# The RWKV recurrence: its triangular solver's data in another DRAM order, block tiles that serve four ticks, and loads issued ahead of output stores

## The chip, the cores and the metric

One Trainium2 chip, one of its cores. The metric is the device time of the whole program in microseconds (us), the median of three runs. The core has five engines with a queue each: TensorE (PE, with its weight loads PEld), VectorE (DVE), ScalarE (ACT), GpSimd (POOL) and SyncE (SP), which here only issues DMAs. Each queue runs in order, and an instruction that waits holds up all that stand behind it.

## The reference

A two-layer trunk: RWKV-7 time mixing and a mixture of experts, then differential attention and a second mixture of experts. Only the time mixing is touched. Its core, for each of 16 heads, is a recurrence over 1024 tokens with a 64x64 state:

```python
def step(S, inp):
    r_t, w_t, k_t, v_t, a_t, b_t = inp
    sa = jnp.einsum('bhij,bhj->bhi', S, a_t)
    S = S * w_t[:, :, None, :] + sa[..., None] * b_t[:, :, None, :] + v_t[..., None] * k_t[:, :, None, :]
    return S, jnp.einsum('bhij,bhj->bhi', S, r_t)
_, y = lax.scan(step, S0, (tm(r_h), tm(w_h), tm(k_h), tm(v_h), tm(a_vec), tm(b_vec)))
```

after which y is normalised by head, gets a bonus term, is multiplied by a gate and by `w_o`.

## The kernel before

The recurrence is computed in chunks of 64 tokens. Two heads stand on the 128 partitions as a pair (p = 0 to 7); two pairs make a couple (four of them, c or g below). Within a chunk the recurrence needs the inverse of a triangular 64x64 matrix I - A for every head and chunk. A is split into 32x32 blocks: the inverses D of the two diagonal blocks come from a forward substitution (the solver), and the block C below the diagonal is used as it is, in three products s1, s2, s3 (Q = D X, P2 = C Q, R = D P2 + Q).

Two stages follow one another, written out by hand in one order for all engines (`tc.manual_schedule()`, L1453), so every queue holds its instructions in the order in which the code is written.

*The k stage* (`rwkv_k`, loop over n at L1455, about 300 to 560 us): 16 units of one pair and half the tokens each. Iteration n makes projections for unit n, norms for unit n - 1, and for unit n - 2 the matrices: `prods` (PE, tile `pA`, from `at` and `bk`) and `mask` (DVE, tile `am`). A unit's `am` holds A (stored to `d['A']`, L1578) and a second matrix (L1579). `ei` (stored to `d['rt']`, L1547 and L1549), `bk` (stored at L1533) and `am` have one buffer each, so each store has to be done before the next unit writes the tile. Four DMAs on POOL's queue fill `d['D']` with zeros ahead of the stage (L1408).

*The recurrence* (`Mix.main`, loop over n at L801, about 526 to 910 us): 32 ticks (and two to drain), each of them two chunks of one couple, eight ticks to a couple. Its first two ticks are interleaved with the last two iterations of the k stage (`mb.step`). Tick n issues `first(n)` (products with the tile `rec`, 768 KB, and with `rI`), `turn(n)`, s1 to s5 for tick n - 1, and the serial `chain(n - 2)`. At its end the loads for tick n + 2 are issued on SP: `rec` and four DMAs for the C blocks (`bdC`) in `load`, `bdD` in `load_t`, `rI` in `load_r`. `gn` normalises finished outputs, from tick 6 on, two pieces in four ticks: on PE, ACT, DVE and twice on POOL (L788, L790, tile `gyc`), and ends with a store to `d['y']` (L797).

*The solver* (`solve_gen`) is a generator, of which a few steps at a time are woven into the order (`mb.solve`, `self.solve`). For couple g it loads A from DRAM with 8 DMAs (L592), so that each of the 128 partitions holds one 32x32 block for 8 of the 16 (head, chunk) places, runs 62 small instructions (L601, L604), on DVE for couple 0 and on POOL for 1 to 3, and stores D with 8 DMAs (L611):

```python
nc.sync.dma_start(a[q0:q0 + 16], src[r:r + 32, :, 32 * b:32 * b + 32].rearrange("i u j -> u i j"))
eng.tensor_mul(tv, a[:, s + 1:, s:s + 1].to_broadcast([P, n, s + 1]),
                     t[:, s:s + 1, :s + 1].to_broadcast([P, n, s + 1]))
```

In the k stage only couple 0 is solved (`mb.solve(.., 1)`); couple 1 begins in tick 0, and `self.solved` at n % 8 == 6 makes sure that a couple is through before its ticks come.

Of the kernel before, what the change touches and what calls it, by code (L numbers as in the profile page):

```python
# [18 lines left out]
P = 128  # L19
# [524 lines left out]
class Mix:  # L544
# [32 lines left out]
    def solve_gen(self, g, eng):  # L577


        nc, d, sp = self.nc, self.d, self.sp  # L580
        B = 32
        for _ in range(3):
            yield
        a = sp.tile([P, B, B], F32, name="big", bufs=3)
        t = sp.tile([P, B, B], F32, name="big", bufs=3)
        for y in range(2):
            src = d['A'][g][:, y]
            for b in range(2):
                for h in range(2):
                    q0 = 64 * y + 32 * b + 16 * h  # L590
                    r = 64 * h + 32 * b
                    nc.sync.dma_start(a[q0:q0 + 16], src[r:r + 32, :, 32 * b:32 * b + 32].rearrange("i u j -> u i j"))  # L592
        nc.gpsimd.memset(t, 0.0)
        for _ in range(9):
            yield
        eng.memset(t.rearrange("p i j -> p (i j)")[:, 0:B * B:B + 1], 1.0)
        for s in range(B - 1):
            n = B - 1 - s
            tmp = sp.tile([P, 256], F32, name="so_tmp", bufs=2)
            tv = tmp[:, :n * (s + 1)].rearrange("p (i j) -> p i j", j=s + 1)  # L600
            eng.tensor_mul(tv, a[:, s + 1:, s:s + 1].to_broadcast([P, n, s + 1]),  # L601
                                 t[:, s:s + 1, :s + 1].to_broadcast([P, n, s + 1]))
            yield
            eng.tensor_add(t[:, s + 1:, :s + 1], t[:, s + 1:, :s + 1], tv)  # L604
            yield
        for y in range(2):
            for b in range(2):
                for h in range(2):
                    q0 = 64 * y + 32 * b + 16 * h
                    o = slice(64 * y + 32 * b, 64 * y + 32 * b + 32)  # L610
                    nc.sync.dma_start(d['D'][g][o, h, :, 32 * b:32 * b + 32].rearrange("i u j -> u i j"), t[q0:q0 + 16])  # L611
        yield

    def main(self):
# [58 lines left out]
        def first(n):  # L673
# [6 lines left out]
            t = qp.tile([P, 8, 2 * L], F32, name="XK", bufs=3)  # L680
# [86 lines left out]
        def gn(p, th):  # L767
# [3 lines left out]
            if th == 0:  # L771
                g2[p] = wp.tile([P, P], F32, name=f"g2{p % 2}", bufs=2)
# [6 lines left out]
            yc = wp.tile([P, 512], F32, name="gyc")  # L779
# [125 lines left out]
class Kern:  # L905
# [237 lines left out]
    def rwkv(self, x, A, rows, ada_first, ada_rest, x_rd, moe, em):  # L1143
# [12 lines left out]
        d['A'] = couples('A', [P, 2, NCH, L])  # L1156
        d['D'] = couples('D', [P, 2, NCH, L])
# [231 lines left out]
    def rwkv_k(self, A, d, wp, front, Z, W2, half, kah, col, PLs, sel2, sel8, strict, X, W, strip, mb):  # L1389
# [5 lines left out]
        with ExitStack() as e1:  # L1395
# [59 lines left out]
            if True:  # L1455
                for n in range(18):
# [107 lines left out]
                    mb.solve(solving, 1)  # L1564
# [12 lines left out]
                    if c:  # L1577
                        nc.sync.dma_start(d['A'][pc_ // 2][:, pc_ % 2, 8 * thc:8 * thc + 8, :], c['am'][:, 0])  # L1578
# [599 lines left out]
```

## Time and profile before

| | us |
|---|---|
| median of three runs | 3038.64 |
| the three runs | 3037.49, 3038.64, 3048.1 |
| the profiled execution, its own time | 3041.39 |
| its span (first to last instruction) | 3039.7 |

Over the span PE is busy for 2669.4 us (88%), DVE for 2295.2 (76%), ACT for 1596.5 (53%), POOL for 1050.4 (35%). These shares are averages over stages with different limits; the change is in one stage of some 600 us. A timeline row gives the start in us, the length in us, the engine, the source line, the operation, the tile written and the tiles read, and in brackets how long the engine had been idle and what released it. "acc<-rI,rec" marks the first matmuls of a tick, so the distance between two such rows is a tick's length.

### The profile page before, as it was taken

How to read it: one execution, taken by the hardware profiler on the slowest of the kernel's cores; microseconds unless marked ns; L12 is line 12 of the kernel's file. 1: busy time of each engine (PE TensorE's matmuls, PEld its weight loads, DVE VectorE, ACT ScalarE, POOL GpSimd, SP SyncE). 2: the span in 40 equal slices, each digit the busy share in tenths (PEclk: the TensorE clock that was granted, in tenths of full speed). 3: DMA queues.
4: the chain of work that ended last, by engine and by line, in shares of the span. 5: the costliest groups of instructions: out<-in, count | busy, mean ns of one | idle time of the engine just before them, and what ended most of it. 6: DMA issues, size and time to landing. Idle time of an engine off the chain costs nothing. (4 is left out here: it accounts for less than half of the span.)

```text
span 3039.7 us, 47397 instructions
## 1 busy us (share of the span) xinstructions
PE 2669.4 (88%) x18150; PEld 2088.7 (69%) x18150; DVE 2295.2 (76%) x3328; ACT 1596.5 (53%) x2105; POOL 1050.4 (35%) x786
## 2 busy tenths in 40 slices
PE   6999998588879699999996789989979799999994
PEld 3567766555658588888774577767758688888773
DVE  7895688345555699999996457676687799999996
ACT  5653433244432177777774244444533377777773
POOL 2000554554332222332223537676242223222320
PEclk9999888789998799999998699999989799999997
DMA  7486765755645499999996113233135499999994
GB/s 263 150 266 215 221 184 166 171 139 148 181 122 196 160 369 380 379 373 367 371 365 216 48 39 99 71 92 98 36 117 199 177 376 379 375 376 374 370 366 175
DMA packets 356952, 696.79 MB, mean 229 GB/s; under 512 B 113336, under 2 KB 231408, under 8 KB 307568
## 3 DMA queue, kind: packets, MB, share of 16 engines
q1 hardware_dynamic: 330144, 649.59, 60.9%
q0 software_dynamic: 22080, 42.00, 5.5%
q8 instruction: 145, 2.38, 0.3%
q10 hardware_dynamic: 4496, 2.12, 0.3%
q14 instruction: 87, 0.71, 0.1%
HBM read 612.71 MB, written 110.15 MB: 238 GB/s over the span
## 5 line engine op out<-in xcount | busy, mean ns | idle before, releaser
L1116 DVE TENSOR_TENSOR elo<-eraw,ehi 128x2048 fp32r<-128x2048 f32 x384 | 871.4, 2286 | 73.6 <-ACT ehi L1113 73.2
L1113 ACT ACTIVATE ehi<-eraw 128x2048 fp32r<-128x2048 f32 x384 | 736.0, 1920 | 178.4 <-PE eacc L350 76.5
L393 POOL DMA_INDIRECT x<-ey,gtab x64 | 205.2, 3206 | 842.4 <-DVE ey L388 831.9
L350 PE MATMUL eacc<-ehi,xTl 128*128 128x512 f32 x1024 | 293.0, 398 | 0.0
L350 PE MATMUL eacc<-ehi,xTh 128*128 128x512 f32 x1024 | 284.1, 399 | 5.8 <-ACT ehi L1113 5.8
L350 PE MATMUL eacc<-elo,xTh 128*128 128x512 f32 x1024 | 277.9, 393 | 0.0
L350 PEld LDWEIGHTS eacc<-elo,xTh 128*128 128x128 f32 x1024 | 193.1, 189 | 43.3
L350 PEld LDWEIGHTS eacc<-ehi,xTh 128*128 128x128 f32 x1024 | 188.8, 190 | 44.0 <-ACT ehi L1113 6.6
L350 PEld LDWEIGHTS eacc<-ehi,xTl 128*128 128x128 f32 x1024 | 188.9, 189 | 38.0
L1771 PE MATMUL acc<-axh,w_hi 128*128 128x512 f32 x384 | 172.9, 450 | 8.1 <-ACT axh L1113 5.5
L1771 PE MATMUL acc<-axl,w_hi 128*128 128x512 f32 x384 | 156.9, 409 | 0.0
L1771 PE MATMUL acc<-axh,w_lo 128*128 128x512 f32 x384 | 156.1, 406 | 0.0
L1892 ACT ACTIVATE pr<-sc,mx 128x128 f32<-128x128 f32 (+7 forms) x128 | 94.1, 739 | 83.4 <-DVE mx L1878 41.6
L378 PE MATMUL ey<-elo,dTh 128*128 128x512 f32 x496 | 133.9, 392 | 0.0
L378 PE MATMUL ey<-ehi,dTh 128*128 128x512 f32 x496 | 133.7, 391 | 0.0
L378 PE MATMUL ey<-ehi,dTl 128*128 128x512 f32 x496 | 133.7, 391 | 0.0
L397 POOL DMA_INDIRECT xg<-hbuf,gtab x64 | 118.3, 1848 | 33.7 <-issue 17.7
L378 PEld LDWEIGHTS ey<-elo,dTh 128*128 128x128 f32 x496 | 93.2, 188 | 20.4
L378 PEld LDWEIGHTS ey<-ehi,dTl 128*128 128x128 f32 x496 | 93.0, 188 | 20.4
L378 PEld LDWEIGHTS ey<-ehi,dTh 128*128 128x128 f32 x496 | 93.2, 188 | 20.2
L1649 POOL TENSOR_TENSOR xres<-xres,wotmp 128x512 f32<-128x512 f32 x32 | 47.4, 1484 | 160.8 <-DVE wotmp L1648 109.4
L1113 ACT ACTIVATE dTh<-etr 128x512 fp32r<-128x512 f32 x64 | 38.3, 598 | 122.9 <-PE etr L369 122.9
(493 smaller groups left out, 6175.6 us busy)
## 6 DMA issues: line engine op xcount, KB each, us to landing
eraw<-in_moe_w_gate_dram SPq DMA_DIRECT2D x128, 1024.0 KB
eraw<-in_moe_w_up_dram SPq DMA_DIRECT2D x128, 1024.0 KB
eraw<-in_moe_w_down_dram SPq DMA_DIRECT2D x128, 1024.0 KB
big<-in_ada_w_dram SPq DMA_DIRECT2D x64, 512.0 KB
rec<-d_rec SPq DMA_DIRECT2D x32, 768.0 KB
xres<-in_ada_w_dram SPq DMA_DIRECT2D x32, 512.0 KB
w_raw<-in_rw_w_rkv_dram SPq DMA_DIRECT2D x24, 512.0 KB
big<-in_ada_kv_w_dram SPq DMA_DIRECT2D x16, 512.0 KB
```

The lines of the kernel that those rows point to most:

```text
L350: self.nc.tensor.matmul(a, lhsT=x_[:, 4 * i + k, :], rhs=w_[:, k, :], start=(i == 0 and n == 0), stop=(i == 1 and n == 11))
L378: self.nc.tensor.matmul(ya[e], lhsT=x_[:, 2 * c + k, :], rhs=w_[:, 2 * k + e, :], start=(c == 0 and n < 2), stop=(c == 1 and n >= 10))
L393: self.nc.gpsimd.indirect_dma_start(out=self.xbuf, out_offset=bass.IndirectOffsetOnAxis(ap=col, axis=0), in_=y, in_offset=None, bounds_che ...
L397: self.nc.gpsimd.indirect_dma_start(out=xg, out_offset=None, in_=self.hbuf, in_offset=bass.IndirectOffsetOnAxis(ap=col, axis=0), bounds_ch ...
L1113: nc.scalar.activation(hi, src, AF.Copy)
L1116: nc.vector.tensor_sub(lo, src, hi.bitcast(F32))
L1649: eng.tensor_add(xt[:, e], xt[:, e], tmp)
L1771: nc.tensor.matmul(acc, lhsT=a[:, kd, :], rhs=y[:, kd, ts], start=(i == 0), stop=(i == 3 * KD - 1))
L1892: nc.scalar.activation(pr[j][:, :n], scs[j][:, :n], AF.Exp, bias=mx[:, j:j + 1], scale=0.125, accum_out=l[:, j:j + 1])
```

## The change

- The solver's input is written to a DRAM tensor of its own, `d['S']`, in the order in which the solver holds it. In the k stage each unit therefore stores A a second time, with four DMAs of 32x8x32 elements (runs of 128 B); the solver then reads its 512 KB with one DMA, and writes D with one, in the same order.
- The products s1 to s3 read D and C from tiles that hold four ticks (`bdD`, `bdC`, two of each, cleared once on POOL), which `blocks` fills with four and two DMAs of runs of 128 B. The zero fill of `d['D']` goes, and so do the loads of `bdD` and `bdC` in every tick.
- Couple 1 may be solved from iteration 14 of the k stage on; for couples 1 to 3 the store of D stands six solver steps later.
- Stores of the normalised output are kept back until the tick's loads are issued, one of them until the next tick. `gyc` has three buffers, `XK` two (before: three), each `g2` tile one (two).

```diff
-        for y in range(2):
-            src = d['A'][g][:, y]
...
-                    nc.sync.dma_start(a[q0:q0 + 16], src[r:r + 32, :, 32 * b:32 * b + 32].rearrange("i u j -> u i j"))
+        nc.sync.dma_start(a.rearrange("p i j -> p (i j)"), d['S'][g])
...
-                    nc.sync.dma_start(d['D'][g][o, h, :, 32 * b:32 * b + 32].rearrange("i u j -> u i j"), t[q0:q0 + 16])
+        for _ in range(6 if g else 0):
+            yield
+        nc.sync.dma_start(d['D'][g], t.rearrange("p i j -> p (i j)"))
...
+        Ds, Cs = ([cp.tile([P, 2, 8, L], F32, name=f"bd{x}{i}", bufs=1) for i in range(2)] for x in "DC")
...
+        for t in Ds + Cs:
+            nc.gpsimd.memset(t, 0.0)
...
-                for s in range(2):
-                    nc.sync.dma_start(Cs[n % 3][o, s, :, 0:32], d['A'][c][o, s, u, 0:32])
-
-        def load_t(n):
-            Ds[n] = cp.tile([P, 2, 2, L], F32, name="bdD")
-            nc.sync.dma_start(Ds[n], d['D'][n // 8][:, :, 2 * (n % 8):2 * (n % 8) + 2, :])
+        def blocks(g):
+            c, th = g // 2, g % 2
+            for y in range(2):
+                for b in range(2):
+                    q0, o = 64 * y + 32 * b + 16 * th, slice(64 * y + 32 * b, 64 * y + 32 * b + 32)
+                    nc.sync.dma_start(Ds[th].rearrange("p s u l -> p (s u) l")[o, :, 32 * b:32 * b + 32],
+                                      d['D'][c][q0:q0 + 16].rearrange("u (i j) -> i u j", j=32))
+                    yield
+            for h in range(2):
+                o = slice(64 * h + 32, 64 * h + 64)
+                nc.sync.dma_start(Cs[th].rearrange("p s u l -> p (s u) l")[o, :, 0:32],
+                                  d['A'][c][o, th, :, 0:32])
+                yield
...
             if p < 7:
-                nc.sync.dma_start(d['y'][p][:, s], yc)
+                kept.append((d['y'][p][:, s], yc))
+                if k > 5:
+                    stores()
...
-            t = qp.tile([P, 8, 2 * L], F32, name="XK", bufs=3)
+            t = qp.tile([P, 8, 2 * L], F32, name="XK", bufs=2)
...
+        def stores(n=0):
+            while len(kept) > n:
+                nc.sync.dma_start(*kept.pop(0))
...
                     load(1)
                     load_r(1)
-                    load_t(1)
+                    for _ in blocks(0):
+                        pass
-                if i == 2 and n + 2 < 32:
-                    if n % 8 == 6:
-                        self.solved((n + 2) // 8)
+                if n % 4 == 2 and i == 0 and n < 30:
+                    self.solved((n + 2) // 8)
+                    parts = blocks(n // 4 + 1)
+                if n % 4 in (2, 3) and i in (2, 4, 6) and n < 28:
+                    next(parts)
...
                         load(n + 2)
-                        load_t(n + 2)
                         load_r(n + 2)
+                    stores(1)
...
-            for c in range(4):
-                nc.gpsimd.dma_start(d['D'][c].rearrange("p s u l -> p (s u l)").rearrange("p (a b) -> p a b", b=8 * P),
-                                    zero[:, None, :].to_broadcast([P, 2, 8 * P]))
...
-                            mb.solve(1, 1)
+                            mb.solve(1, 1 if n < 14 else 2)
...
-                        nc.sync.dma_start(d['A'][pc_ // 2][:, pc_ % 2, 8 * thc:8 * thc + 8, :], c['am'][:, 0])
+                        for h in range(2):
+                            for b_ in range(2):
+                                q0, r = 64 * (pc_ % 2) + 32 * b_ + 16 * thc + 8 * h, 64 * h + 32 * b_
+                                nc.sync.dma_start(d['S'][pc_ // 2][q0:q0 + 8].rearrange("u (i j) -> i u j", j=32),
+                                                  c['am'][r:r + 32, 0, :, 32 * b_:32 * b_ + 32])
+                        nc.sync.dma_start(d['A'][pc_ // 2][:, thc, 8 * (pc_ % 2):8 * (pc_ % 2) + 8], c['am'][:, 0])
```

PE's, DVE's and ACT's queues hold the same instructions in the same order in both kernels. SP's and POOL's differ, at three places that matter below (line numbers in the rows of the changed kernel are its own; `rec`, `rI`, `bdD`, `bdC` are the tiles of the ticks, `big` the solver's, `d_D_105` and `d_D_109` couple 1's D).

First, SP where couple 1 has been solved. Before, the store of D (`d_D_105`, 8 DMAs) stands between the loads for ticks 5 and 6, with the 8 loads of the next couple's A behind it:

```order
L642 DMA rec<-d_rec_92 128x12x128
L647 DMA bdC_4660<-d_A_100 32x2x32 x4
L651 DMA bdD<-d_D_104 128x2x128
L654 DMA rI_4658<-d_rt_96 128x8x64
L611 DMA d_D_105<-big 16x32x32 x8
L592 DMA big<-d_A_102 16x32x32 x8
L642 DMA rec<-d_rec_92 128x12x128
L647 DMA bdC_4652<-d_A_100 32x2x32 x4
L651 DMA bdD<-d_D_104 128x2x128
L654 DMA rI_4650<-d_rt_96 128x8x64
```

Now the store (`d_D_109`) stands between the loads for ticks 4 and 5, among the block loads for ticks 4 to 7:

```order
L633 DMA rec<-d_rec_92 128x12x128
L655 DMA rI_4698<-d_rt_96 128x8x64
L642 DMA bdD_4693<-d_D_108 32x16x32
L602 DMA d_D_109<-big 128x1024
L647 DMA bdC_4695<-d_A_100 32x16x32
L586 DMA big<-d_S_106 128x1024
L633 DMA rec<-d_rec_92 128x12x128
L655 DMA rI_4700<-d_rt_96 128x8x64
```

Here 16 DMAs of the solver became two, and the place moved ahead by one tick.

Second, POOL at the seam of the two stages. Before, the products of units 14 and 15 (`bk`, `k`) have the memset of the solver's result and four solver instructions between them:

```order
L1471 TENSOR_TENSOR bk<-k_4573,en 128x512
L1472 TENSOR_TENSOR k_4573<-k_4573,r 128x512
L1525 TENSOR_TENSOR k_4696<-k_4696,k 128x512
L593 MEMSET big 128x1024
L596 MEMSET big 128x32
L601 TENSOR_TENSOR so_tmp<-big 128x31
L604 TENSOR_TENSOR big<-big,so_tmp 128x31
L601 TENSOR_TENSOR so_tmp<-big 128x60
L604 TENSOR_TENSOR big<-big,so_tmp 128x30x2
L1471 TENSOR_TENSOR bk<-k_4696,en 128x512
L1472 TENSOR_TENSOR k_4696<-k_4696,r 128x512
```

Now there are five whole memsets ahead, and 22 solver instructions between the two `bk`:

```order
L587 MEMSET big 128x1024
L627 MEMSET bdD_4692 128x1024
L627 MEMSET bdD_4693 128x1024
L627 MEMSET bdC_4694 128x1024
L627 MEMSET bdC_4695 128x1024
L1480 TENSOR_TENSOR bk<-k_4611,en 128x512
L1481 TENSOR_TENSOR k_4611<-k_4611,r 128x512
L1534 TENSOR_TENSOR k_4738<-k_4738,k 128x512
...
L595 TENSOR_TENSOR so_tmp<-big 128x231
L598 TENSOR_TENSOR big<-big,so_tmp 128x21x11
L1480 TENSOR_TENSOR bk<-k_4738,en 128x512
L1481 TENSOR_TENSOR k_4738<-k_4738,r 128x512
```

The solver's input load for couple 1 has moved with it: it now stands on SP right behind the store of unit 13's `bk`, before it stood behind the loads for tick 1.

Third, SP at the end of each unit of the k stage. Before:

```order
L1549 DMA d_rt_98<-ei 64x4x128 x2
L1578 DMA d_A_102<-am 128x512
L1579 DMA d_rec_94<-am 128x512
L1426 DMA r<-d_r_90 128x512
L1416 DMA w_raw<-in_rw_w_rkv_dram 128x8x128
```

and now:

```order
L1558 DMA d_rt_98<-ei 64x4x128 x2
L1590 DMA d_S_106<-am 32x8x32 x4
L1592 DMA d_A_102<-am 128x512
L1593 DMA d_rec_94<-am 128x512
L1435 DMA r<-d_r_90 128x512
L1425 DMA w_raw<-in_rw_w_rkv_dram 128x8x128
```

Four more DMAs in each unit, ahead of the store of A.

## Rows read from the trace of the kernel before

**Rows 1.** PE waits, 526 to 912 us: engine line <- releaser, total us, times, longest

```profile
PE acc L663 <- DMA rI<-d_rt: 27.9, 3, 18.8
```

**Rows 2.** SyncE's queue: its waits, 380 to 912 us

```profile
SPq L797 <- DVE gyc L794: 58.8, 12, 12.1
...
SPq L1515 <- ACT en L1517: 36.0, 10, 6.0
...
SPq L611 <- POOL big L604: 16.1, 3, 12.5
```

**Rows 3.** PE timeline: start us, us, operation, [idle before <- releaser]; a tick's first matmuls

```profile
554.13 1.76 PE L1433 MATMUL pA<-bk,at 64*64 64x128 f32 x14 [4.42 <-POOL bk L1471]
...
575.39 1.10 PE L663 MATMUL acc<-rI,rec 64*64 64x128 f32 x32
...
582.60 1.10 PE L663 MATMUL acc<-rI,rec 64*64 64x128 f32 x32
...
608.59 1.98 PE L663 MATMUL acc<-rI,rec 64*64 64x128 f32 x32 [18.80 <-DMA rI<-d_rt]
...
621.65 1.99 PE L663 MATMUL acc<-rI,rec 64*64 64x128 f32 x32
...
631.53 1.05 PE L663 MATMUL acc<-rI,rec 64*64 64x128 f32 x32
...
675.70 1.98 PE L663 MATMUL acc<-rI,rec 64*64 64x128 f32 x32 [5.07 <-DMA rI<-d_rt]
```

**Rows 4.** PE timeline around the third stall

```profile
735.62 1.99 PE L663 MATMUL acc<-rI,rec 64*64 64x128 f32 x32 [4.04 <-DMA rI<-d_rt]
```

**Rows 5.** SyncE's queue, timeline, 577 to 662 us

```profile
577.90 0.55 SPq L654 DMA_DIRECT2D rI<-d_rt  x1
...
591.03 4.80 SPq L611 DMA_DIRECT2D d_D<-big  x8
...
595.87 4.50 SPq L592 DMA_DIRECT2D big<-d_A  x8
...
600.47 0.53 SPq L642 DMA_DIRECT2D rec<-d_rec  x1
...
604.31 0.55 SPq L654 DMA_DIRECT2D rI<-d_rt  x1
...
656.25 5.64 SPq L611 DMA_DIRECT2D d_D<-big  x8
```

**Rows 6.** Granted clock (column after POOL), DMA share, GB/s inside the first stall

```profile
598.00:600.00 2.00, 0.00 (x0) 0.00 (x0) 0.00 (x0) 0.00 (x0) 0.00 (x0) 0.50 0.76 124
```

**Rows 7.** POOL timeline, 520 to 640 us

```profile
530.97 0.95 POOL L593 MEMSET big<- 128x1024 f32 x1
...
551.50 0.25 POOL L601 TENSOR_TENSOR so_tmp<-big 128x31 f32<-128x31 f32 x1 [19.37 <-DMA big<-d_A]
...
552.81 1.26 POOL L1471 TENSOR_TENSOR bk<-k,en 128x512 f32<-128x512 f32 x1
...
565.29 0.64 POOL L604 TENSOR_TENSOR big<-big,so_tmp 128x231 f32<-128x231 f32 x1
...
590.75 0.25 POOL L604 TENSOR_TENSOR big<-big,so_tmp 128x31 f32<-128x31 f32 x1
...
604.44 0.25 POOL L601 TENSOR_TENSOR so_tmp<-big 128x31 f32<-128x31 f32 x1 [12.33 <-DMA big<-d_A]
...
626.03 1.27 POOL L788 TENSOR_TENSOR gyc<-gyc,gsq 128x512 f32<-128x512 f32 x1 [8.15 <-ACT P L715]
```

**Rows 8.** DVE timeline, 525 to 535 us

```profile
529.87 2.08 DVE L1055 TENSOR_SCALAR nr_y<-nr_i 128x8 int32<-128x8 int32 x1
```

**Rows 9.** DMA queue while only D is stored, 592 to 596 us: packets, MB, share

```profile
q1 hardware_dynamic: 3207, 0.40, 79.3%
```

**Rows 10.** ACT timeline, 315 to 320 and 515 to 520 us

```profile
318.31 0.63 ACT L1511 ACTIVATE ei<-cum 128x512 f32<-128x512 f32 x1 [4.09 <-DMA d_rt<-ei]
...
519.95 0.63 ACT L1511 ACTIVATE ei<-cum 128x512 f32<-128x512 f32 x1 [3.33 <-DMA d_rt<-ei]
```

More of the change, by code (lines that the diff above doesn't have):

```diff
@@ L585, in solve_gen @@
         t = sp.tile([P, B, B], F32, name="big", bufs=3)
-        for y in range(2):
-            src = d['A'][g][:, y]
[L588 to L591, printed above, removed]
-                    nc.sync.dma_start(a[q0:q0 + 16], src[r:r + 32, :, 32 * b:32 * b + 32].rearrange("i u j -> u i j"))
+        nc.sync.dma_start(a.rearrange("p i j -> p (i j)"), d['S'][g])
         nc.gpsimd.memset(t, 0.0)
@@ L605, in solve_gen @@
             yield
[L606 to L610, printed above, removed]
-                    nc.sync.dma_start(d['D'][g][o, h, :, 32 * b:32 * b + 32].rearrange("i u j -> u i j"), t[q0:q0 + 16])
+        for _ in range(6 if g else 0):
+            yield
+        nc.sync.dma_start(d['D'][g], t.rearrange("p i j -> p (i j)"))
         yield
@@ L625, in main @@
         self.solved(0)
-        rI, Cs, rec, Ds = [], [], {}, {}
+        rI, rec = [], {}
+        Ds, Cs = ([cp.tile([P, 2, 8, L], F32, name=f"bd{x}{i}", bufs=1) for i in range(2)] for x in "DC")
         def forms():
@@ L631, in forms @@
             rI.append(r)
-            c = cp.tile([P, 2, 2, L], F32, name=f"bdC{len(Cs)}", bufs=1)
-            nc.gpsimd.memset(c, 0.0)
-            Cs.append(c)
         for _ in range(3):
             forms()
+        for t in Ds + Cs:
+            nc.gpsimd.memset(t, 0.0)
         def load(n):
-            c, u = n // 8, slice(2 * (n % 8), 2 * (n % 8) + 2)
+            c = n // 8
             t = cp.tile([P, 12, 2 * L], F32, name="rec")
@@ L643, in load, with block @@
             rec[n] = t.rearrange("p (k s) (u l) -> p k s u l", s=2, l=L)
+        def blocks(g):
[6 more added lines that the diff above has]
+                    yield
             for h in range(2):
                 o = slice(64 * h + 32, 64 * h + 64)
-                for s in range(2):
-                    nc.sync.dma_start(Cs[n % 3][o, s, :, 0:32], d['A'][c][o, s, u, 0:32])
-        def load_t(n):
-            Ds[n] = cp.tile([P, 2, 2, L], F32, name="bdD")
-            nc.sync.dma_start(Ds[n], d['D'][n // 8][:, :, 2 * (n % 8):2 * (n % 8) + 2, :])
+                nc.sync.dma_start(Cs[th].rearrange("p s u l -> p (s u) l")[o, :, 0:32],
+                                  d['A'][c][o, th, :, 0:32])
+                yield
+        def block(t, n):
+            return lambda r, c, u: t[n // 4 % 2][r, c, 2 * (n % 4) + u]
         def load_r(n):
@@ L723, in s1 @@
         def s1(n):
-            copied(n, 'Q', quad(of(Ds[n]), of(q[n]['X'])))
+            copied(n, 'Q', quad(block(Ds, n), of(q[n]['X'])))
         def s2(n):
-            copied(n, 'P2', quad(of(Cs[n % 3]), of(q[n]['Q'])))
+            copied(n, 'P2', quad(block(Cs, n), of(q[n]['Q'])))
         def s3(n):
-            added(n, 'R', quad(of(Ds.pop(n)), of(q[n]['P2'])), flat(q[n]['Q']), 1)
+            added(n, 'R', quad(block(Ds, n), of(q[n]['P2'])), flat(q[n]['Q']), 1)
         def s4(n):
@@ L771, in gn @@
             if th == 0:
-                g2[p] = wp.tile([P, P], F32, name=f"g2{p % 2}", bufs=2)
+                g2[p] = wp.tile([P, P], F32, name=f"g2{p % 2}", bufs=1)
                 nc.sync.dma_start(g2[p], w_g2[:, p * P:(p + 1) * P])
@@ L778, in gn @@
             nc.scalar.activation(sq, pc, AF.Square)
-            yc = wp.tile([P, 512], F32, name="gyc")
+            yc = wp.tile([P, 512], F32, name="gyc", bufs=3)
             nc.scalar.activation(yc, pc, AF.Copy)
@@ L796, in gn @@
             if p < 7:
-                nc.sync.dma_start(d['y'][p][:, s], yc)
+                kept.append((d['y'][p][:, s], yc))
+                if k > 5:
+                    stores()
+        kept = []
+        def stores(n=0):
+            while len(kept) > n:
+                nc.sync.dma_start(*kept.pop(0))
         load(0)
         load_r(0)
-        load_t(0)
         yield
@@ L867, in main @@
             pass
+        stores()
         self.part = list(part)[-1]
@@ L1155, in rwkv @@
         d['rt'] = couples('rt', [P, 8, 2, 2, 2 * L])
-        d['A'] = couples('A', [P, 2, NCH, L])
-        d['D'] = couples('D', [P, 2, NCH, L])
+        d['A'] = couples('A', [P, 2, 16, L])
+        d['S'] = couples('S', [P, 1024])
+        d['D'] = couples('D', [P, 1024])
         with ExitStack() as es:
@@ L1563, in rwkv_k @@
                         pq = prods(c, 1)
-                    mb.solve(solving, 1)
+                    mb.solve(solving, 1 if n < 14 else 2)
                     if c:
```

## The prediction

> **What bounds the kernel now.** I first read who waits for whom in the recurrence, then PE's timeline there, then the queues behind its longest gaps. Over 526 to 912 us PE names a DMA as releaser three times only, always `rI`, the last load of a tick: 27.9 us, the longest 18.8 [rows 1]. The three are in front of ticks 6, 12 and 18 (18.80, 5.07 and 4.04 us) [rows 3, 4]. Elsewhere a tick is a chain of work between PE, DVE, ACT and POOL: 7.2 us without the normalisation (575.39 to 582.60), 9.9 with it (621.65 to 631.53) [rows 3].
>
> The first gap has its cause on SP. After the loads for tick 5 (577.90) SP issues nothing until 591.03: the store of couple 1's D waits for the solver's last instruction on POOL (590.75) [rows 5, 7]; of SP's 16.1 us in this wait 12.5 are here [rows 2]. Then 8 stores (4.80 us) and 8 loads of the next couple's A (4.50) are issued, and only then tick 6's loads, `rec` at 600.47 and `rI` at 604.31; PE starts at 608.59, 4.3 us after that [rows 3, 5]. Meanwhile the granted clock has fallen to 0.50 [rows 6], the lower level (1.2 GHz), with PE idle, and tick 6 takes 13.06 us. At the next couple POOL is nearly in time and the issue alone does the harm: 5.64 us for the stores from 656.25 on, eight loads behind them, then 5.07 us of idle PE [rows 3, 5].
>
> **The change part by part.** The sum is made against the profiled execution: 3041.39 us, span 3039.7 and 1.7 around it, 2.75 above the median of 3038.64.
>
> *Removed, the stalls.* 16 DMAs of 0.56 to 0.71 us become two at each couple, so ticks 12 and 18 lose their cause: -5.1 and -4.0. Tick 6 loses 18.8 if the store comes in time (below). The half-clock ticks behind them: tick 6 13.06 against 9.88 for tick 7 [rows 3], -3.2; the other two restart alike (1.98 and 1.99 for the first matmuls, 1.10 at the higher level) after a shorter idle time, and I take 2 for each. Together -35.1.
>
> *Couple 1 on POOL, earlier.* Before, the solver stands idle for 19.37 us until its input lands (551.50), and unit 15's `bk`, four solver instructions behind, holds PE back by 4.42 us (554.13) [rows 3, 7]. Now the load stands ahead of those for tick 0, and the input has landed when POOL comes. POOL gets there after four more whole memsets (0.95 each [rows 7]) in place of three quarter-size ones: about 3 us later than 531.9, so 535. Of the 62 instructions 22 come before `bk`; they took 551.50 to 565.93 less the two products of 1.26 and their gaps (2.6), 11.8 us. `bk` starts at about 546.7 instead of 552.8. PE could then go on at 549.7, where its gap began: up to -4.4. I take -3: the block loads for ticks 0 to 3 are issued behind those of tick 1, and s1 may wait for them. The remaining 40 instructions (565.93 to 591.00, 25.1 us) end at 549.3 + 25.1 = 574.4.
>
> *The wait that is left.* The D store still waits for POOL, now in tick 3, and the loads for tick 5 are behind it. From 574.4 on SP issues the store, two C blocks, the next input and `rec` (five DMAs of about 0.56), `rI` at 577.2; with 4.3 to landing, 581.5. Tick 5 began at 582.60 and would now begin 3 earlier, 579.6. Cost +2, with 0 to 6 as bounds (POOL 4 us sooner or later).
>
> *POOL in tick 7.* Couple 2 starts on POOL when its input lands, about 575.5 + 4.3 = 580. The first `gyc` product now stands behind 45 of its instructions (order of the changed kernel); at 36.9 / 62 = 0.6 us each that is 607. By the trace `gyc` is wanted 4.4 us after tick 7's start (626.03 against 621.65) [rows 3, 7]; tick 7 would start at 581.5 + 7.2 + 9.9 = 598.6, so at 603. POOL is 4 us late, DVE's product with `gyc` behind it, and in DVE's queue the additions that PE waits for. Cost +4, bounds 0 and 8. Afterwards 12 instructions per tick (7.2 us) and one `gyc` product of 1.27 fit into 9.9.
>
> *The k stage.* 64 more DMAs on SP, four per unit, 0.56 each as the loads of 128 B runs took (4.50 / 8) [rows 5]: 2.2 us per unit. Cover: in 10 units SP waited 36.0 us for ACT's `en`, 3.6 per unit [rows 2]. On the DMA engines: while only D was stored, 3207 packets of 128 B took 79.3% of 16 engines for 4 us [rows 9], 15.8 ns each, so a unit's 1024 packets fill all 16 for 1.0 us. Cost 0. Without cover it is 2.2 + 1.0 = 3.2 for each of 16 units, 51. On the other side the zero fill and the 8 D stores ahead of unit 14's `rt` stores go, and ACT waited 4.09 and 3.33 us for just these [rows 10]; PE was not idle for it, so I take 0, at most -7.4.
>
> The Trainium skill (DMA: Bandwidth & Descriptors, section Specifications) says that below 512 B a transfer does not reach line rate, since the engine reads, modifies and writes. The rate in rows 9, 0.40 MB in 4 us, agrees, and it speaks against the four stores per unit; by it alone the outcome would be the rival of the k stage below.
>
> *Memsets at the seam.* While POOL runs there, DVE's 128x8 conversion took 2.08 us from 529.87 on, to the end of the memset of 530.97 [rows 7, 8]. Now the four extra memsets meet DVE's three copies of `eye`. Cost +1, bounds 0 and 3.
>
> The skill (SBUF — State Buffer, section SBUF: two separate sides) calls it an exclusive lock on a shared port pair, held for a whole instruction. Rows 8 look like it; by that rule the worst would be each copy waiting out one memset, 3 x 0.95 = 2.9 us, as an estimate, and the sum would be 2 higher.
>
> *At nothing.* Block tiles: six DMAs in four ticks replace 20, with 3072 packets instead of 2048; 1024 x 15.8 ns / 16 = 1 us in four ticks in which DMA waits have vanished. They are issued one to three ticks ahead; late by 1 us in each of eight groups they would cost 8. Stores kept back: SP's 58.8 us in front of them [rows 2] delay loads, but PE names no DMA outside the three gaps, so 0. `XK` with two buffers is written only after a tick's first matmuls (1.10 [rows 3]), and the last read of the old one stands ahead of them; were half a us missing, 32 ticks would give 16. `g2`: the old reader is four ticks back.
>
> Sum: -35.1 - 3 + 2 + 4 + 1 = -31, so 3010 by the profiled execution and 3007.6 by the median. I forecast 3008.
>
> **The rivals.** *The solver isn't earlier.* If POOL and DVE hold each other up over the 22 instructions, or the input lands late in the traffic at the seam, the store waits as before; only the issue shrinks, from 9.3 to about 1.1 us. Then tick 6 keeps some 10.6 of its 18.8 and its slow clock; -8.2, -9.1 and -4 for the others make -21: 3017. For it: the store's place moved ahead by a tick, against the solver. Against it: 16 us of earlier start.
>
> *POOL sets the ticks.* With the stalls gone, POOL's lag doesn't drain, and `gyc` comes 5 us late in all six pieces of ticks 6 to 17 instead of 4 in one: +26, which eats most of the gain: 3034. For it: POOL needs 8.5 of 9.9 us in a tick. Against it: from 604.44 to 626.03 it had 8.15 us of idle time [rows 7].
>
> *The k stage pays.* The small stores stand in front of the next unit's stores in the DMA queues, and `ei`, `bk` and `am`, with one buffer each, wait for them; 3.2 us per unit, 16 units, +51 - 31: 3059, slower than before. It decides from 2 us per unit on. For it: waits of 3.33 and 4.09 us for just such stores exist [rows 10]. Against it: those were behind 4096 packets or 4 MB, not 1024 packets.
>
> *More than that.* The seam's store waits are on the path too (-7), POOL isn't late in tick 7 (-4), and lighter SP traffic takes 0.2 us off each of 26 ticks (-5): 2992. Against it: no PE wait names these.
>
> **How the numbers follow.** Forecast 55% (2999 to 3014), solver not earlier 17%, POOL sets the ticks 14%, more than that 8%, the k stage 6%. The range of 2994 to 3026 takes in the first two, most of the gain rival and little of the others, about 80%. A measurement of this kernel can tell 0.5%, 15 us, from no change: faster is below 3023.4, which the forecast, the late solver and the larger gain give, 80%; the same 14%; slower 6%.
>
> **What would show it.** Right: no idle PE time over 3 us in front of ticks 6, 12 and 18, a granted clock that stays at the higher level from tick 2 to 20; the solver's first instruction on POOL at about 535 and its 62nd at about 574; SP's longest wait for POOL under 8 us; iterations of the k stage as long as before. A DVE wait for POOL's `gyc` of about 4 us in tick 7 would show that term. Wrong: PE waiting for `am`, `bk` or `ei` stores in the k stage, PE waits for block loads, or `gyc` waits in every tick.

## The result and the profile after

The changed kernel took 3000.7 us (median of four, 2992.9 to 3005.4), the kernel before 3039.2 in the same session: ratio 0.987, 95% interval 0.985 to 0.989. 38.5 us were gained where 31 were forecast. The profiled executions differ by 36: 3005.44 against 3041.39.

Where these 36 us lie shows on DVE's timeline. A tick's `XK` product follows its first matmuls by 1.8 to 2.1 us in the ticks shown (3 in tick 0), so it marks the ticks; the rows are the last scan of the k stage and the marks of ticks 4, 20 and 31. Before:

```profile
516.60 1.23 DVE L1507 TENSOR_TENSOR_SCAN cum<-rst,tw 128x512 f32<-128x512 f32 x1
...
577.19 0.69 DVE L682 TENSOR_TENSOR XK<-acc,m_incl 128x512 f32<-128x512 f32 x1 [1.66 <-ACT XK L681]
...
758.54 0.69 DVE L682 TENSOR_TENSOR XK<-acc,m_incl 128x512 f32<-128x512 f32 x1 [2.14 <-ACT XK L681]
...
863.77 0.69 DVE L682 TENSOR_TENSOR XK<-acc,m_incl 128x512 f32<-128x512 f32 x1 [0.80 <-ACT XK L681]
```

And after:

```profile
520.11 1.23 DVE L1516 TENSOR_TENSOR_SCAN cum<-rst,tw 128x512 f32<-128x512 f32 x1
...
576.91 0.69 DVE L683 TENSOR_TENSOR XK<-acc,m_incl 128x512 f32<-128x512 f32 x1 [2.50 <-ACT XK L682]
...
725.88 0.69 DVE L683 TENSOR_TENSOR XK<-acc,m_incl 128x512 f32<-128x512 f32 x1 [1.94 <-ACT XK L682]
...
825.02 0.69 DVE L683 TENSOR_TENSOR XK<-acc,m_incl 128x512 f32<-128x512 f32 x1 [0.80 <-ACT XK L682]
```

The differences: up to the last scan +3.5, the seam and ticks 0 to 3 -3.8, ticks 4 to 19 -32.4, ticks 20 to 30 -6.1, behind that +2.7; together -36.

PE's timeline at the ticks that stood behind the three stalls [rows 3, 4], and at tick 5 (start, us, operation, idle before and releaser):

```profile
575.12 1.10 PE L664 MATMUL acc<-rI,rec 64*64 64x128 f32 x32 [0.78 <-DMA rI<-d_rt]
...
587.66 1.99 PE L664 MATMUL acc<-rI,rec 64*64 64x128 f32 x32 [5.27 <-DMA rI<-d_rt]
...
596.38 1.10 PE L664 MATMUL acc<-rI,rec 64*64 64x128 f32 x32
...
651.12 1.09 PE L664 MATMUL acc<-rI,rec 64*64 64x128 f32 x32
...
705.63 1.10 PE L664 MATMUL acc<-rI,rec 64*64 64x128 f32 x32
```

Ticks 6, 12 and 18 (596.38, 651.12, 705.63) start with no idle time and at the higher clock. One stall is new, 5.27 us ahead of tick 5, with the 1.99 us of the lower level behind it. SP's timeline shows its cause:

```profile
570.11 1.32 SPq L642 DMA_DIRECT2D bdD<-d_D  x1
576.92 0.34 SPq L602 DMA_DIRECT2D d_D<-big  x1
577.31 0.59 SPq L647 DMA_DIRECT2D bdC<-d_A  x1
577.95 0.71 SPq L586 DMA_DIRECT2D big<-d_S  x1
578.71 0.46 SPq L647 DMA_DIRECT2D bdC<-d_A  x1
579.27 0.54 SPq L633 DMA_DIRECT2D rec<-d_rec  x1
579.90 2.12 SPq L655 DMA_DIRECT2D rI<-d_rt  x1
```

The granted clock, 1.00 up to the stall, is 0.50 from 587 to 592 us. SP stands at the store of D until 576.92; tick 5's `rec` is issued at 579.27 and its `rI` at 579.90, and PE goes on 7.8 us after that. POOL, which the store waits for, and its later rows:

```profile
535.36 0.48 POOL L595 TENSOR_TENSOR so_tmp<-big 128x31 f32<-128x31 f32 x1
...
548.19 1.27 POOL L1480 TENSOR_TENSOR bk<-k,en 128x512 f32<-128x512 f32 x1
...
576.65 0.25 POOL L598 TENSOR_TENSOR big<-big,so_tmp 128x31 f32<-128x31 f32 x1
...
611.09 1.27 POOL L789 TENSOR_TENSOR gyc<-gyc,gsq 128x512 f32<-128x512 f32 x1
```

The solver begins 16 us earlier [rows 7] and ends 14 us earlier, and the idle time of 4.42 us for `bk` [rows 3] is gone. The first `gyc` product comes 4.1 us after tick 7's start (606.99), about as before (4.4).

### The profile page after: what moved, and what is told of

It is laid out like the page before. It is cut to its first block, busy times and chain, and to the rows that moved or that the text cites. A ratio compares the mean times of both kernels' runs of the same rounds, so it can differ in the third digit from the quotient of the medians.

```text
span 3003.7 us, 47206 instructions
## 1 busy us (share of the span) xinstructions
PE 2659.4 (89%) x18150; PEld 2080.2 (69%) x18150; DVE 2303.1 (77%) x3328; ACT 1596.0 (53%) x2105; POOL 1059.7 (35%) x783
## 5 line engine op out<-in xcount | busy, mean ns | idle before, releaser
L1127 DVE TENSOR_TENSOR elo<-eraw,ehi 128x2048 fp32r<-128x2048 f32 x384 | 871.2, 2286 | 74.8 <-ACT ehi L1124 73.5
L393 POOL DMA_INDIRECT x<-ey,gtab x64 | 209.6, 3276 | 837.0 <-DVE ey L388 826.4
```

What stands on the lines that cost most here:

```text
L393: self.nc.gpsimd.indirect_dma_start(out=self.xbuf, out_offset=bass.IndirectOffsetOnAxis(ap=col, axis=0), in_=y, in_offset=None, bounds_che ...
L1127: nc.vector.tensor_sub(lo, src, hi.bitcast(F32))
```

## The experiments

Twelve kernels; each edit is to the changed kernel unless it says so. Executions of one kernel differ by 5 to 25 us, so medians settle only large effects; the smaller ones are read from stretches of the profiled execution, by the marks above (us):

| kernel | median, ratio to before (95%) | first to last scan | last scan to tick 4 | 4 to 20 | 20 to 31 | tick 0 to 31 |
|---|---|---|---|---|---|---|
| before | 3039.2 | 211.8 | 60.6 | 181.4 | 105.2 | 326.6 |
| changed | 3000.7, 0.985 to 0.989 | 212.6 | 56.8 | 149.0 | 99.1 | 283.0 |
| late_start | 2996.3, 0.983 to 0.987 | 212.1 | 57.8 | 150.0 | 98.3 | 283.3 |
| late_start_no_delay | 3010.1, 0.986 to 0.993 | 212.4 | 59.3 | 156.9 | 99.1 | 293.1 |
| early_alone | 3041.1, 0.999 to 1.002 | 214.7 | 74.8 | 163.6 | 104.9 | 318.1 |
| store_from_pool | 3001.1, 0.985 to 0.990 | 213.7 | 56.4 | 152.1 | 98.3 | 284.9 |
| store_behind_load | 3000.6, 0.985 to 0.990 | 212.0 | 58.9 | 148.2 | 100.8 | 285.9 |
| direct_y | 3000.6, 0.985 to 0.991 | 210.1 | 56.8 | 150.6 | 99.8 | 285.0 |
| four_more_loads | 2998.5, 0.985 to 0.989 | 208.3 | 56.2 | 150.3 | 98.7 | 283.4 |
| direct_y_and_loads | 3002.3, 0.985 to 0.988 | 209.6 | 56.3 | 149.9 | 100.9 | 285.5 |
| seam_on_act | 2995.6, 0.982 to 0.991 | 213.7 | 56.0 | 151.1 | 98.6 | 285.3 |
| small_stores_twice | 3004.0, 0.983 to 0.991 | 216.4 | 63.8 | 146.0 | 98.2 | 286.3 |
| seam_store_pace | 3000.3, 0.983 to 0.987 | 210.2 | 63.3 | 143.7 | 98.5 | 284.3 |
| pace_on_sp | 2992.3, 0.980 to 0.985 | 212.5 | 56.0 | 143.4 | 99.0 | 277.7 |

**What removed the stall of tick 6: late_start, late_start_no_delay, early_alone.**

```diff
-                            mb.solve(1, 1 if n < 14 else 2)
+                            mb.solve(1, 1)
-                    mb.solve(solving, 1 if n < 14 else 2)
+                    mb.solve(solving, 1)
```

> The changed kernel, but couple 1 starts on POOL where it did before (its input is asked for after tick 0's loads). Theory A (the forecast's account: the earlier start removes the wait for POOL, the single DMAs remove only the issue): SP waits over 10 us for POOL's last solver instruction, PE stands idle 8 to 12 us on rI ahead of one tick between 5 and 8, the granted clock falls there, and the time is 8 to 14 us above the changed kernel, 3009 to 3015. Rival B (single DMAs and their place do it all): no PE idle over 6 us on a DMA, at most 3 us above, 3001 to 3004.

Rival B held; the median even lies 5 us below its range. SP's timeline:

```profile
580.60 2.11 SPq L655 DMA_DIRECT2D rI<-d_rt  x1
588.53 0.34 SPq L602 DMA_DIRECT2D d_D<-big  x1
588.92 0.42 SPq L586 DMA_DIRECT2D big<-d_S  x1
589.44 1.87 SPq L633 DMA_DIRECT2D rec<-d_rec  x1
```

The solver ends nearly as late as in the kernel before, and the store goes out at 588.53: 2.5 us sooner than before [rows 5], 11.6 us later than in the changed kernel. But with the later start and the six extra solver steps it stands behind the `rI` of tick 6 (580.60); behind it are only loads for tick 7 and later ones. SP waited 5.7 us there, and PE's largest wait for `rI` in the whole recurrence was 0.5. So the six steps were taken out of late_start:

```diff
-        for _ in range(6 if g else 0):
+        for _ in range(0):
             yield
```

> The run late_start without the six extra solver steps ahead of the D store: couple 1's D store now stands on SP between tick 5's and tick 6's loads (as in the kernel before), no longer behind tick 6's. Theory A (the store's place in SP's queue decides: whatever load stands behind a store that waits for POOL is late): PE idle 5 to 11 us on a DMA ahead of tick 6 with matmuls at the lower clock behind it, the recurrence (tick 0 to 31) 6 to 12 us longer than late_start's 283.3, 3002 to 3008. Rival B (one DMA in place of 16 removes the stall wherever it stands): no PE idle over 3 us ahead of tick 6, recurrence within 2 us of 283.3.

Theory A held: the store is one place earlier on SP, between the loads of ticks 5 and 6:

```profile
575.00 1.01 SPq L655 DMA_DIRECT2D rI<-d_rt  x1
590.67 0.34 SPq L602 DMA_DIRECT2D d_D<-big  x1
591.07 0.42 SPq L586 DMA_DIRECT2D big<-d_S  x1
591.59 0.74 SPq L633 DMA_DIRECT2D rec<-d_rec  x1
592.42 1.14 SPq L655 DMA_DIRECT2D rI<-d_rt  x1
```

PE's first matmuls of tick 6 there:

```profile
599.73 1.98 PE L664 MATMUL acc<-rI,rec 64*64 64x128 f32 x32 [8.39 <-DMA rI<-d_rt]
```

The stall is back, 8.39 us, and ticks 0 to 31 are 9.8 us longer than in late_start (the median, 3010.1, is 2 us above the range given).

This run also tells why the stalls of ticks 12 and 18 went. Without the six steps the stores of couples 2 and 3 stand again ahead of the loads for ticks 12 and 18, as in the kernel before. For tick 18 the store goes out 7.0 us into tick 16 in both. SP in the kernel before, then SP and PE in late_start_no_delay:

```profile
722.10 5.32 SPq L611 DMA_DIRECT2D d_D<-big  x8
```

```profile
705.84 0.32 SPq L602 DMA_DIRECT2D d_D<-big  x1
```

```profile
715.25 1.10 PE L664 MATMUL acc<-rI,rec 64*64 64x128 f32 x32
```

With one DMA in place of eight, tick 18 starts with no idle time (before: 4.04 us [rows 4]); tick 12 does too. At these two fewer DMAs were enough, as the forecast has it.

Third, the early start by itself, in the kernel before:

```diff
-                            mb.solve(1, 1)
+                            mb.solve(1, 1 if n < 14 else 2)
-                    mb.solve(solving, 1)
+                    mb.solve(solving, 1 if n < 14 else 2)
```

> The kernel before with one edit: couple 1 may start on POOL during the last units, as in the changed kernel; 16 small DMAs a couple stay. Theory A: the 12.5 us wait goes and the issue of 9.3 stays, so the gap of 18.8 shrinks to 6 to 10 us, ticks 12 and 18 keep 5.07 and 4.04; 8 to 14 us below the kernel before, 3025 to 3031. Rival B: the issue alone makes the gap, nothing is gained, 3036 to 3041.

Theory A fell, and rival B's time came, though not by its reason: SP still waited 11.7 us for POOL. PE's waits, 526 to 912 us:

```profile
PE acc L663 <- DMA big<-d_A: 16.0, 1, 16.0
...
PE acc L663 <- DMA rI<-d_rt: 7.9, 1, 7.9
...
PE acc L663 <- DMA bdD<-d_D: 3.9, 1, 3.9
```

The solver was earlier, and so was the store's place: it moved from ahead of tick 6's loads to ahead of tick 4's, which are at 582.57 and 586.28 in SP's rows:

```profile
577.55 4.92 SPq L611 DMA_DIRECT2D d_D<-big  x8
582.57 0.65 SPq L642 DMA_DIRECT2D rec<-d_rec  x1
...
586.28 0.55 SPq L654 DMA_DIRECT2D rI<-d_rt  x1
```

A stall of 16.0 us ahead of tick 4 (PE names a load of `big`, which its matmuls do not read) replaces 18.8, and one of 7.9 ahead of tick 10 replaces 5.07 and 4.04. Ticks 0 to 31 gained 8.5 us, but tick 0 begins 4.6 us later behind the last scan, since the eight loads of couple 1's input (4.84 us on SP) now stand ahead of the seam's stores and loads.

**The stall that is left, and POOL: store_from_pool, store_behind_load.**

```diff
-        for _ in range(6 if g else 0):
-            yield
-        nc.sync.dma_start(d['D'][g], t.rearrange(...))
+        (nc.gpsimd if g else nc.sync).dma_start(d['D'][g], t.rearrange(...))
```

> The changed kernel, but the D stores of couples 1 to 3 are issued by POOL behind the solver's last instruction, not by SP, so no load stands behind them. Theory A (the gap ahead of tick 5 is the SP wait for POOL that is left): the 5.27 us gap and the slow matmuls behind it go, 5 to 8 us below the changed kernel, 2993 to 2996. Rival B (the loads take 7.7 us to land since the block loads fill the DMA engines): a gap of 3 to 5 us on rI stays ahead of tick 5, 0 to 2 us gained. Rival C (issuing costs POOL a microsecond or more, and gyc comes late): DVE waits over 20 us for POOL's gyc, no gain.

```diff
-        for _ in range(6 if g else 0):
+        for _ in range(24 if g else 0):
```

> The changed kernel with 24 extra solver steps ahead of the D store in place of 6: couple 1's D store stands behind tick 5's loads. Theory A (the 5.27 us gap ahead of tick 5 is the store's place, and nothing takes its turn): the gap goes, recurrence 276 to 279 against 283.0. Rival B (POOL's lag sets ticks 5 to 9: a stall at tick 5 only gives POOL time, and where it goes POOL's gyc is late instead): the gap goes, but PE or DVE waits 3 to 5 us for gyc, st or P in ticks 7 to 9, recurrence 282 to 285, as in store_from_pool (284.9) and late_start.

In both the gap ahead of tick 5 is gone, and neither gained: theory A saw the cause of the gap and missed what follows it. PE in store_from_pool, then in store_behind_load (tick 9 and, alike, tick 17):

```profile
615.52 0.49 PE L662 MATMUL py<-m_eye,st 64*64 64x64 f32 x8 [3.82 <-ACT st L753]
```

```profile
624.12 1.13 PE L664 MATMUL acc<-P,bdD 64*64 64x128 f32 x16 [2.51 <-ACT P L716]
...
698.58 0.67 PE L664 MATMUL acc<-P,bdD 64*64 64x128 f32 x16 [2.91 <-ACT P L716]
```

`st` and `P` are copies on ACT; they stand behind ACT's scaling of `gyc`, which waits for POOL's product (6.25 us in store_from_pool), and that stands behind the solver's instructions. The kernel before has this wait too, 2.28 us in its tick 9. In the changed kernel PE names none ahead of tick 13; I read this as POOL catching up during the stall of tick 5.

**The shorter ticks 20 to 31: direct_y, four_more_loads, direct_y_and_loads.**

```diff
-                kept.append((d['y'][p][:, s], yc))
-                if k > 5:
-                    stores()
+                nc.sync.dma_start(d['y'][p][:, s], yc)
```

> The changed kernel, but each d_y store is issued at its product, ahead of the tick's loads, as before. Theory A (the forecast's zero for this edit): SP waits some 40 to 60 us for DVE's gyc products, PE does not notice, the time is that of the changed kernel, 3000 plus or minus 3, ticks 20 to 31 are as long. Rival B (the stores kept back made the ticks shorter that the forecast priced at nothing): 5 to 10 us above, 3005 to 3011, of them about 6 in ticks 20 to 31.

```diff
+        pad = cp.tile([P, 2, 2, 32], F32, name="pad", bufs=1)
         def load(n):
...
+            if n > 20:
+                for h in range(2):
+                    o = slice(64 * h + 32, 64 * h + 64)
+                    for s in range(2):
+                        nc.sync.dma_start(pad[o, s], d['A'][c][o, s, 2 * (n % 8):2 * (n % 8) + 2, 0:32])
```

> The changed kernel; from tick 21 on each tick loads four more 32x128 B pieces into an unused tile between its rec and rI, as the kernel before did for bdC. Theory A (ticks 20 to 31 are shorter after the change since SP issues five fewer DMAs a tick, so the w_o piece behind them is issued sooner, POOL converts it sooner, and gyc behind that in POOL's queue isn't late): ticks 20 to 31 take 102 to 106 us instead of 99.1, PE waits 2.5 to 3.1 us for ACT's P twice, POOL waits 36 us or more for w_o instead of 31.8. Rival B (three gyc buffers or the block tiles themselves made it): 98.5 to 100.5 us as now.

> The changed kernel with both earlier edits at once: each d_y store issued at its product, ahead of the tick's loads, and four more 32x128 B loads in each tick from tick 21 on. Each alone left ticks 20 to 31 at 98.7 to 99.8 us (before: 105.2). Theory A (the two together made the longer ticks: SP waits for gyc, then issues five DMAs more, and the w_o piece behind them comes late by both): 103 to 106 us, POOL waits 36 us or more for w_o, PE waits 2 to 3 us for ACT's P at least twice. Rival B (it is the third gyc buffer, or the block tiles themselves): 98.5 to 101 us.

 (both edits)

Why these ticks were longer before is seen in one of them. SP in the kernel before, tick 28 (its first matmuls at 830.96):

```profile
829.74 0.33 SPq L797 DMA_DIRECT2D d_y<-gyc  x1
...
830.74 3.75 SPq L647 DMA_DIRECT2D bdC<-d_A  x4
...
835.97 0.52 SPq L1588 DMA_DIRECT2D big<-in_rw_w_o_dram  x1
```

POOL in the kernel before waits for this piece of `w_o`, and `gyc` stands behind its conversion:

```profile
842.16 1.04 POOL L1595 CAST wo_hi<-big 128x1024 fp32r<-128x1024 f32 x1 [9.75 <-DMA big<-in_rw_w_o_dram]
845.59 1.26 POOL L788 TENSOR_TENSOR gyc<-gyc,gsq 128x512 f32<-128x512 f32 x1
```

PE then waits 3.11 us for ACT's `P` at 848.23. In the changed kernel the piece is issued 0.9 us after tick 28's start, not 5.0:

```profile
797.40 0.38 SPq L1602 DMA_DIRECT2D big<-in_rw_w_o_dram  x1
```

Rebuilt on the changed kernel, neither the early store (99.8 us) nor four more loads (98.7) nor both together (100.9) bring back the 105.2; kernels without either edit lie between 98.2 and 100.8. With both edits the eight pieces of `w_o` are issued 3.5 us into their ticks on average (before 3.7, changed 2.4), so the later issue was rebuilt on the whole, but not at the tick read above: 2.7 us into tick 28, before 5.0. That SP's later issue alone made these ticks longer is thus not borne out, and for tick 28 not excluded. The chain is read from the trace; what keeps it short in the changed kernel is not settled. The block tiles and the other buffer counts (`gyc`, `XK`, `g2`), which all three kept, were not tried alone.

**The seam: seam_on_act.**

```diff
-            nc.vector.tensor_copy(r.rearrange(...)[:, :, 0, :], eye[:, None, :].to_broadcast([P, 8, L]))
+            nc.scalar.activation(r.rearrange(...)[:, :, 0, :], eye[:, None, :].to_broadcast([P, 8, L]), AF.Copy)
```

> The changed kernel with the three copies of eye into rI on ACT, which is idle there, instead of on DVE. Theory A (DVE's copies took 5.19 us instead of 1.08 since POOL's memsets of the block tiles run beside them, and DVE's next unit and PE's pA behind it are late by as much): PE's idle of 7.3 us ahead of pA becomes 2.5 to 4.5, and from the last scan of the k stage to tick 0 the time is 3 to 5 us shorter; total 2996 to 2998. Rival B (pA waits for POOL's bk behind the same memsets): PE idle 6 to 7.3 us, 0 to 1 us shorter.

In the changed kernel DVE's three copies are:

```profile
528.87 5.19 DVE L622 COPY rI<-m_eye 128x512 f32<-128x512 f32 x3
```

Only the first copy ran beside memsets. By itself it is

```profile
528.87 2.39 DVE L622 COPY rI<-m_eye 128x512 f32<-128x512 f32 x1
```

and ends at 531.26, 0.3 us after the last memset (530.98). The second and the third end at 532.66 and 534.06, again 0.3 us after an instruction of POOL, its products `bk` and `k`:

```profile
530.94 1.43 POOL L1480 TENSOR_TENSOR bk<-k,en 128x512 f32<-128x512 f32 x1
532.45 1.33 POOL L1481 TENSOR_TENSOR k<-k,r 128x512 f32<-128x512 f32 x1
```

PE's gap behind the copies:

```profile
537.58 1.76 PE L1442 MATMUL pA<-bk,at 64*64 64x128 f32 x14 [7.30 <-DVE pn L1079]
```

With the copies on ACT, PE's timeline is:

```profile
533.67 1.97 PE L1442 MATMUL pA<-bk,at 64*64 64x128 f32 x16 [4.92 <-DVE pn L1079]
...
547.93 1.59 PE L664 MATMUL acc<-XK,bdD 64*64 64x128 f32 x13 [3.39 <-DMA bdD<-d_D]
```

PE's gap shrinks by 2.4 us, less than expected; tick 0 comes 1.5 us earlier, and s1 then waits for the D pieces, which SP issues as late as before. Up to tick 4 0.8 us is left: between the theories.

**The k stage: small_stores_twice.**

```diff
                                 nc.sync.dma_start(d['S'][pc_ // 2][q0:q0 + 8]..., c['am'][r:r + 32, 0, :, 32 * b_:32 * b_ + 32])
+                                nc.sync.dma_start(d['S2'][pc_ // 2][q0:q0 + 8]..., c['am'][r:r + 32, 0, :, 32 * b_:32 * b_ + 32])
```

> The changed kernel with each of the four S stores of a unit issued a second time, into a tensor that nothing reads: 64 more DMAs of 128 B runs in the k stage. Theory A (cost nothing, as the forecast had it, since SP and the DMA engines have room in a unit): first to last scan 208 to 214 us as in the ten runs so far (211.8 before), total 2996 to 3003. Rival B (a unit has no more room: SP's 2.2 us or the engines' 1.0 us per unit show): 10 to 51 us more in the k stage, 3010 or above, with waits of ACT or DVE for stores of ei, bk or am.

Inconclusive by its time. First to last scan is 216.4 us, 3.8 above the changed kernel (0.24 per unit) and 1.7 above the longest of the others. The seam pays 7: its three units' stores stand on SP ahead of tick loads, with PE waits of 2.73 us for `bdD` and 3.81 for `rI`. The first four stores cost nothing that shows: 208 to 214 us in the eleven traces that have them, 211.8 and 214.7 in the two without.

**A faster version: seam_store_pace, pace_on_sp.** Both take the copies on ACT, hold couple 1's store alone back by 24 steps, slow the solver in ticks 4 to 9, and move the first block loads:

```diff
-        for _ in range(6 if g else 0):
+        for _ in range((0, 24, 6, 6)[g]):
...
-                self.solve(2 if n < 6 else 1 + i % 2)
+                self.solve(2 if n < 4 else 1 if n < 10 else 1 + i % 2)
```

> A candidate for a faster version, of four edits to the changed kernel: the copies of eye on ACT; couple 1's D store behind tick 5's loads (24 extra solver steps for that couple alone); one solver step per piece instead of two in ticks 4 and 5, and instead of one and a half in ticks 6 to 9, so that POOL comes to gyc earlier; the block loads for ticks 0 to 3 issued by ACT, not behind tick 1's loads on SP. Theory A (what is left around ticks 4 to 10 is POOL's lag and the place of the store): no PE idle over 2 us in ticks 4 to 12, tick 0 to 31 in 274 to 278 us instead of 283, and 1 to 4 us less ahead of tick 4; total 2988 to 2994. Rival B (POOL's work in ticks 4 to 16 is the bound whatever its order): a wait for gyc or for a D block appears in a later tick, 281 to 285 us, total 2996 to 3002.

Ticks 4 to 20 came out as theory A has it, 143.7 us with no PE wait over 2 us in ticks 4 to 12, but the six loads issued on ACT kept its own work waiting: 5.55 and 2.82 us of issue, and PE idle for 9.10 us on `blkr`. In pace_on_sp SP issues them again, the D pieces ahead of tick 1's loads:

```diff
-                    load(1)
-                    load_r(1)
-                    for _ in blocks(0):
+                    parts = blocks(0)
+                    for _ in range(4):
+                        next(parts)
+                    load(1)
+                    load_r(1)
+                    for _ in parts:
                         pass
```

> The candidate again with the block loads of ticks 0 to 3 back on SP, the four D pieces now ahead of tick 1's loads and the two C pieces behind them; the other three edits of seam_store_pace stay (copies of eye on ACT, couple 1's D store behind tick 5's loads, fewer solver steps in ticks 4 to 9). Theory A (the 9 us that PE waited for ACT's blkr in seam_store_pace came from the six DMAs issued on ACT, and the pace of the solver gives 5 us in ticks 4 to 20): from the last scan of the k stage to tick 4 54 to 57 us (63.3 in seam_store_pace, 56.8 in the changed kernel), ticks 4 to 20 143 to 145 us (149.0 in the changed kernel), total 2992 to 2997. Rival B (what is gained at one place comes back as another wait): the sum from the last scan to tick 20 stays within 2 us of the changed kernel's 205.8, total 2997 to 3003.

Theory A held: 2992.3 us, the fastest of all. Last scan to tick 20 takes 199.4 us, 6.4 less than in the changed kernel; no stall of tick 5, and no PE wait over 1.7 us in ticks 3 to 17. The ratio's interval just overlaps that of the changed kernel (0.980 to 0.985 against 0.985 to 0.989): some 8 us by the medians, not well measured.

## Why the prediction was right, and where it was not

The time and the range held. The terms that make it were not all right, and the reason given for the largest was wrong.

- **Stalls removed, -35.1: size right, reason wrong.** The gaps of 18.8, 5.07 and 4.04 us are gone; ticks 6, 12 and 18, apart from them, are 2.5, 1.6 and 2.5 us shorter, 6.5 where 7.2 were estimated. The step that failed is "tick 6 loses 18.8 if the store comes in time". In late_start the store came only 2.5 us sooner than before, and the stall went all the same; with the store one place earlier 8.39 us of it came back. What decides is which loads stand behind the waiting store. For ticks 12 and 18 the reason given, fewer DMAs, held. The forecast placed the changed store correctly, in tick 3 ahead of tick 5's loads, but credited POOL's earlier end instead of that place.
- **The rival "solver isn't earlier" was mispriced.** It kept 10.6 us at tick 6 and gave 3017. The run with just that condition took 2996.3, since the six extra steps carry the store past tick 6's loads. Without them the stall was 8.39 us.
- **Couple 1 earlier, -3: little of it.** POOL began at 535.36 (535 forecast), `bk` at 548.19 (546.7), and the 62nd instruction was over at 576.9 (574.4). The stretch up to tick 4 is 3.8 us shorter, but 2.8 without the early start, and other kernels with the early start and the same seam lie between 56.2 and 58.9 us (late_start: 57.8). So the early start's own share is not told from noise, and what gives the 2.8 is not shown.
- **The wait that is left, +2: the mechanism right, the size not.** SP waited 5.4 us for POOL, under 8 as forecast. But PE stood 5.27 us, and ticks 4 and 5 together took 21.3 us against 14.4 for two of 7.2: +6.9. POOL was 2.5 us later than worked out, and PE went on 7.8 us after the `rI` issue where 4.3 were taken. The 4.3 was read from one stall in which `rI` was issued 3.8 us behind `rec` (600.47 and 604.31 [rows 5]). Counted from `rec`, the stalls agree: PE goes on 8.1, 8.0 and 8.1 us after it in the three stalls before, 8.4 in tick 5 of the changed kernel, 8.1 in tick 6 of late_start_no_delay. With `rec` issued at 576.6, as the forecast's own sum has it, 8.1 more make 584.7, a cost of 5 instead of 2. In this stall the granted clock fell, so it did not stay high from tick 2 to 20, which the forecast had named as a sign of being right.
- **POOL late in tick 7, +4: 0, and joined to the term above.** The start of `gyc` is 4.1 us into the tick, about as before, and DVE's longest wait for it in ticks 7 to 9 is 2.5 us, not 4. The stall at tick 5 and POOL's lag are one quantity that shows at either place: where the stall went, PE waited 2.5 to 3.8 us for copies behind `gyc`. Taken together +2 and +4 nearly hit the measured +6.9.
- **The k stage, 0: right.** 211.8 us before, 212.6 after, the other kernels around them. The 3.5 us by which the last scan comes later lie mostly (2.7) ahead of the first.
- **Memsets at the seam, +1: about right in the end, not in its parts.** The copies went from 1.08 to 5.19 us and PE's gap there from 5.95 to 7.30. By the lock that the Trainium skill (SBUF — State Buffer, section SBUF: two separate sides) describes, the forecast had estimated 2.9 as the worst; the copies lost 4.1. The trace agrees with a lock held for whole instructions, each copy ending just behind one of POOL's; the estimate was too low, since it counted one memset per copy: the first waited for more than one, and the others for products of 1.43 and 1.33 us.
- **At nothing: wrong by 6 us in ticks 20 to 31.** The rival "more than that" had 0.2 us per tick by lighter traffic on SP, 5 in all. PE's waits of before named no DMA there, which was taken as proof; but the trace leads from PE's wait for `P` over `gyc` and POOL's conversion to a load. That lighter traffic is the reason was not borne out by the runs. Ticks 7 to 19 hold another 4.9 us that no term names (the stalls and the half-clock ticks apart): ticks 9 and 15 are 3.6 and 2.7 us shorter, tick 13 is 2.8 longer. No run tried them alone.

The total was nearer than its parts, and that is in part luck. In the profiled executions the removed stalls gave -34.4 us, the way up to tick 4 -3.8, ticks 4 and 5 +6.9, and the ticks that had been priced at nothing -4.9 and -6.1. Against these 11 us stand 6.2 us outside these stretches (+3.5 ahead of them, +2.7 behind), which lie within the spread of executions.

## What to carry to other kernels

Where one queue issues both stores that wait for a slow engine and loads with a due time, first see which loads stand behind the store. Moving it past one tick's loads took 9.8 us off ticks 0 to 31 (late_start against late_start_no_delay); starting its producer earlier on top of that, which also moved the store forward again, took off nothing more (283.3 against 283.0). A stall that gives a lagging engine time hides that lag: before removing it, ask what the engine does next, and slow or move that work in the same edit. And where PE names ACT or DVE, follow the wait on through the queues: the first cause may be a load two engines away.

## What was not expected of the hardware

- DVE's three copies took 1.08 us with GpSimd all but idle beside them and 5.19 us beside its memsets and products; on ACT, beside the same memsets, they took 1.65.
- In eleven stalls of more than 3 us ahead of ticks 4 to 18, in eight kernels, PE went on 7.9 to 8.7 us after the issue of the tick's `rec`, although `rI` was issued 0.6 us behind it in some and 5.2 in one; in a twelfth (small_stores_twice) it was 7.1.
- Couple 1's store, issued by GpSimd, took 0.79 us of its queue; six loads issued by ACT took 8.4 us of ACT's, where SP needed 6.5.
- Executions of one kernel lay 0.2% to 0.8% apart, lowest to highest; at that spread a gain of 5 us is seen only in the stretches of a trace.
